# Weight bounds over partitions: a way through DRAM and VectorE in place of a GpSimd reduction

## The chip, the cores and the metric

One core of a Trainium2 chip runs the whole kernel. The metric is the device time of one execution in microseconds. The engines are named as in the profile: PE is TensorE's matmul, PEld its weight load, DVE is VectorE, ACT is ScalarE, POOL is GpSimd, SP is SyncE, which here only issues DMAs.

## The reference

A block of a streaming encoder on 2048 tokens of width 1024: a norm, one wide projection, stick-breaking attention and latent attention beside each other, gates, an output projection, and a last norm.

```python
h = rmsnorm(x, norm_in_g[l])
proj = jnp.einsum("bsd,de->bse", h, w_in[l])
(q_sb, k_sb, v_sb, gate_sb, c_q, c_kv, k_rope, gate_mla, gate_logits) = jnp.split(proj, offsets, axis=-1)
o_sb = stick_breaking_attention(q_sb, k_sb, v_sb)
y_sb = jnp.einsum("bsc,cd->bsd", o_sb * jax.nn.silu(gate_sb), w_o_sb[l])
q = jnp.einsum("bsr,re->bse", rmsnorm(c_q, q_norm_g[l]), w_q_up[l])
kv = jnp.einsum("bsr,re->bse", rmsnorm(c_kv, kv_norm_g[l]), w_kv_up[l])
o_mla = chunk_causal_softmax_attention(q_full, k_full, v_mla)
y_mla = jnp.einsum("bsc,cd->bsd", o_mla * jax.nn.silu(gate_mla), w_o_mla[l])
g = jax.nn.sigmoid(gate_logits + b_gate[l])
merged = g[:, :, 0, :] * y_sb + g[:, :, 1, :] * y_mla
x = x + jnp.einsum("bsd,de->bse", merged, w_out[l])
return rmsnorm(x, norm_f_g)
```

Each of the two attentions has 8 heads of width 64; the latent one adds 32 rotated columns to queries and keys.

## The kernel before

Every matrix product is made of three float16 products: each operand is split into a high part and a low part (`split`, L135: ScalarE casts the high part, VectorE takes the difference), and `gemm` (L139) adds high times high, high times low and low times high. Float16 has a narrow range, so each weight block is scaled first. The scale is a power -1/2 of a bound of the block, and the bound must be one number for all 128 partitions.

`prep_w` (L109) prepares one weight block: it loads it in two pieces (L118), ScalarE squares it and sums along the rows (L120), `bound_of` (L94) makes the bound, and then the block is cast into high and low parts with the factor `gs` (L126 to L131). `prep_up` (L391) does the same for the two up-projections of the latent attention, and `tail_scale` (L604) makes only the bound, for the output weights. There are 18 bounds: four of stick-breaking blocks, four of the latent attention (`cq`, `qu`, `ck`, `kvu`), eight of gate blocks, and two of output weights (`wo`, `wout`).

In `bound_of` VectorE sums the partition's squares (L97) and multiplies by the largest squared gain (L99), GpSimd takes the maximum over all partitions (L100), VectorE guards it against zero (L101), GpSimd takes the power -1/2 (L102), and VectorE multiplies the two to the square root (L103). The same power on GpSimd (L92) serves every norm, in `inv_rms`.

The work runs in two streams, which the program interleaves as it is written. `dense_stream` (L643) walks through the projections, block after block, 16 blocks of 128 rows in each; it prepares the next weight block all at once after the third row block (L649). The other stream is the attention: 8 stick-breaking heads (`sb_units`), then 8 latent heads (`mla_units`). `PLAN` says how many row blocks of the dense stream go beside each head: 17 in each of the first eight, 8 in the next seven, 4 in the last. The first 16 row blocks are beside the first norm of the input (`norm_x`). At the end come the gated output projections (L796 on).

A scheduler in the compiler puts the instructions of each engine into an order, by its own estimate of when each is ready; on the chip each engine then takes its queue in that order and waits where something is late. SP's queue holds the weight loads and also the transposes of the attention weights (L254, `hlT` from `hl`), each of which waits for VectorE's low part (L350) and is waited for by TensorE's product with the values (L263). On VectorE the stick-breaking heads bring a scan (L343), a product (L346) and a difference (L350) for each chunk; GpSimd brings the two triangular selects (L334, L336) and the power of the norms, and it issues DMAs.

`normed_ct` (L358) projects to the latent width, and its norm's factor `f` is taken on GpSimd (L92) and then multiplied by `m14`, a multiple of the bound, on VectorE (L366).

Of the kernel before, what the change touches and what calls it, by code (L numbers as in the profile page):

```python
# [9 lines left out]
F32 = mybir.dt.float32  # L10
# [20 lines left out]
SCALES = ("g", 5)  # L31
# [5 lines left out]
def block_kernel(tc, x, norm_in_g, w_in, w_ck, b_gate, q_norm_g, w_q_up, kv_norm_g, w_kv_up,  # L37
# [11 lines left out]
    with ExitStack() as ctx:  # L49
# [44 lines left out]
        def bound_of(ss, g2, m, rm):  # L94
# [14 lines left out]
        def prep_w(src, kk, n, g, g2, name):  # L109
# [15 lines left out]
            bound_of(am[:, 0:kk // 2], g2, m, rm)  # L125
# [22 lines left out]
        with ExitStack() as tctx:  # L148
# [57 lines left out]
            def sb_prep(hp):  # L206
                wh, wl, m = prep_w(w_in[hp], KD, WB, g_in, g2_in, f"sb{hp}")
# [150 lines left out]
            def normed_ct(i, wh, wl, n, nk, m24, m14, cdim):  # L358
# [6 lines left out]
                inv_rms(ssq, 1.0 / cdim, EPS, f)  # L365
                V.tensor_tensor(out=f, in0=f, in1=m14, op=ALU.mult)  # L366
# [24 lines left out]
            def prep_up(w, kk, n, g, g2, name):  # L391
# [15 lines left out]
                bound_of(am[:, 0:2 * kk], g2, m, rm)  # L407
# [14 lines left out]
            def mq_prep():  # L422
                wh, wl, mcq = prep_w(w_in[4], KD, 384, g_in, g2_in, "cq")
                uh, ul, mq = prep_up(w_q_up, 3, 768, g_q, g2_q, "qu")
                m24, m14 = scaled(mcq, 2.0 ** -24, "cq24"), scaled(mcq, 2.0 ** -14, "cq14")
                return wh, wl, uh, ul, mq, m24, m14

            def mq_project(pre):
                wh, wl, uh, ul, mq, m24, m14 = pre
                first = lambda i: normed_ct(i, wh, wl, 384, 3, m24, m14, 384)[1] if i < NB else None  # L430
# [22 lines left out]
            def mk_prep(mq):  # L453
                wh, wl, mck = prep_w(w_ck, KD, 288, g_in, g2_in, "ck")
                uh, ul, mkv = prep_up(w_kv_up, 2, 1024, g_kv, g2_kv, "kvu")
                m24, m14 = scaled(mck, 2.0 ** -24, "ck24"), scaled(mck, 2.0 ** -14, "ck14")
# [12 lines left out]
                return wh, wl, uh, ul, m24, m14, fkn, fkr, mzc, mof  # L469

            def mk_project(pre):
                wh, wl, uh, ul, m24, m14, fkn, fkr = pre[0:8]
                def first(i):
                    if i == NB:
                        return None
                    ps, ct = normed_ct(i, wh, wl, 288, 2, m24, m14, 256)
# [84 lines left out]
            def gate_prep(b):  # L561
                c0 = b * WB
                wh, wl, m = prep_w(w_in[5 + b], KD, WB, g_in, g2_in, f"gt{b}")
# [294 lines left out]
```

## Time and profile before

| | us |
|---|---|
| median of 3 runs (2335.77 to 2342.42) | 2337.99 |
| the profiled execution | 2340.05 |
| its span | 2338.2 |
| PE busy | 1903.0 (81%) |
| DVE busy | 1583.1 (68%) |
| ACT busy | 1241.5 (53%) |
| POOL busy | 483.7 (21%) |

The span is the profiled execution from its first instruction to its last; the time around it is 1.85 us. Busy is the time in which an engine has an instruction under way; waiting, branching and issuing DMAs don't count. In the rows, what stands behind an arrow in square brackets is what ended the idle time before an instruction; "issue" is time in which the engine waited for nothing that the profile shows. PEclk is the granted share of TensorE's full clock.

### The profile page before, as it was taken

To read this page: it belongs to the slowest core of one execution; us is meant where nothing else is said; L and a number is where in the kernel's file an instruction comes from. 1 tells how busy PE (TensorE), PEld (TensorE's weight loads), DVE (VectorE), ACT (ScalarE), POOL (GpSimd) and SP (SyncE) were. 2 spreads that over 40 slices of the span, in tenths; PEclk is the share of its full clock that TensorE was granted. 3 is DMA by queue.
4 is the path that set the end of the run, shared out by engine and by line. 5 is a ranking of instruction groups with operands and counts; after the bars stand their busy time and mean duration, and the time that the engine had idled before them with its cause. 6 is when DMAs were issued, how large, how long until landed. Compare 5 with 4: busy or idle time off the path is not lost.

```text
span 2338.2 us, 41738 instructions
## 1 busy us (share of the span) xinstructions
PE 1903.0 (81%) x15520; PEld 1102.1 (47%) x15520; DVE 1583.1 (68%) x3018; ACT 1241.5 (53%) x2180; POOL 483.7 (21%) x1128
## 2 busy tenths in 40 slices
PE   4677778778876887878887979988798895999997
PEld 2344444444444544545454545555455553444443
DVE  3356677766876866979786766766477667676674
ACT  4454656454565656767664655766456556332221
POOL 1212323322212213342322212211122110000000
PEclk9888989899997989999999989999899897999999
DMA  7976777686998868868676979999999988877752
GB/s 199 217 166 122 157 142 151 123 148 119 188 180 179 177 156 172 168 132 167 132 159 122 196 161 170 219 208 224 178 186 173 219 192 185 237 197 203 201 153 73
DMA packets 918253, 400.48 MB, mean 171 GB/s; under 512 B 857120, under 2 KB 875040, under 8 KB 916000
## 3 DMA queue, kind: packets, MB, share of 16 engines
q1 hardware_dynamic: 895456, 338.53, 71.6%
q0 software_dynamic: 20480, 58.74, 9.4%
q8 instruction: 122, 2.00, 0.4%
q10 hardware_dynamic: 2112, 0.52, 0.1%
q14 instruction: 83, 0.68, 0.1%
HBM read 131.34 MB, written 71.83 MB: 87 GB/s over the span
## 4 chain that ended last, share of the span: by engine, by line
PE 28%; DMA 24%; issue 19%; DVE 16%; ACT 7%; POOL 4%; SPq 2%; POOLq 0%; DVEq 0%; ACTq 0%
DMA hlT<-hl 13%; PE z L307 5%; DVE U L343 4%; DMA rt<-r 4%; PE mm L142 3%; PE mm L143 3%; PE mm L144 3%; DVE B L346 2%; DMA utb<-hlb 2%; DVE hl L350 2%; PE yo L142 2%; PE yo L144 2%; PE yo L143 2%; ACT U L331 1%; PE y L142 1%
## 5 line engine op out<-in xcount | busy, mean ns | idle before, releaser
L142 PE MATMUL mm<-w,hT 128*128 128x384 f16 (+1 forms) x1792 | 604.9, 338 | 118.0 <-DVE r L137 39.8
L143 PE MATMUL mm<-w,hT 128*128 128x384 f16 (+1 forms) x1792 | 605.2, 338 | 0.4 <-DVE w L131 0.4
L144 PE MATMUL mm<-w,hT 128*128 128x384 f16 (+1 forms) x1792 | 604.0, 337 | 0.0
L307 PE MATMUL z<-kt,qt 128*128 128x512 f16 (+3 forms) x1280 | 318.6, 364 | 89.7 <-ACT B L332 31.9
L263 PE MATMUL av<-vt,hlT 128*128 128x64 f16 x2176 | 238.7, 198 | 181.7 <-DMA hlT<-hl 178.7
L343 DVE TENSOR_TENSOR_SCAN U<-U 128x1024 f32<-128x1024 f32 (+3 forms) x192 | 332.1, 1732 | 45.1 <-POOL U L334 33.2
L263 PEld LDWEIGHTS <-hlT 128*128 128x128 f16 x2176 | 202.0, 101 | 237.3 <-DMA hlT<-hl 216.8
L349 ACT CAST hl<-B 128x1024 f16<-128x1024 f32 (+3 forms) x192 | 153.0, 798 | 269.9 <-DVE B L346 165.6
L143 PEld LDWEIGHTS <-hT 128*128 128x128 f16 x1792 | 182.2, 102 | 215.7 <-issue 115.7
L142 PEld LDWEIGHTS <-hT 128*128 128x128 f16 x1792 | 182.5, 102 | 150.6 <-issue 21.3
L307 PEld LDWEIGHTS <-qt 128*128 128x128 f16 x1600 | 147.2, 101 | 214.0 <-issue 85.3
L144 PEld LDWEIGHTS <-hT 128*128 128x128 f16 x1792 | 182.7, 102 | 124.9 <-issue 23.6
L266 PE MATMUL av<-vt,hlT 128*128 128x64 f16 x2176 | 238.2, 197 | 0.0
L265 PE MATMUL av<-vt,hlT 128*128 128x64 f16 x2176 | 238.0, 197 | 0.0
L350 DVE TENSOR_TENSOR hl<-B,hl 128x1024 f16<-128x1024 f32 (+3 forms) x192 | 174.3, 911 | 53.4 <-ACT hl L349 52.9
L265 PEld LDWEIGHTS <-hlT 128*128 128x128 f16 x2176 | 201.6, 101 | 17.4 <-issue 1.7
L266 PEld LDWEIGHTS <-hlT 128*128 128x128 f16 x2176 | 201.9, 101 | 0.0
L346 DVE TENSOR_TENSOR B<-B,U 128x1024 f32<-128x1024 f32 (+3 forms) x192 | 175.5, 916 | 12.9 <-POOL B L336 3.8
L332 ACT ACTIVATE B<-z,zc 128x1024 f32<-128x1024 f32 (+3 forms) x192 | 166.4, 866 | 31.2 <-DVE hl L350 30.8
L331 ACT ACTIVATE U<-z,nzc 128x1024 f32<-128x1024 f32 (+3 forms) x192 | 166.3, 866 | 13.8 <-PE z L307 13.5
L544 ACT ACTIVATE U<-U,nb 128x1024 f32<-128x1024 f32 (+7 forms) x128 | 98.5, 770 | 130.4 <-DVE nb L538 121.8
L92 POOL TENSOR_TENSOR f<-f,mhalf 128x1 f32<-128x1 f32 x64 | 41.6, 653 | 504.7 <-DVE f L91 497.5
(230 smaller groups left out, 3394.1 us busy)
## 6 DMA issues: line engine op xcount, KB each, us to landing
gd<-go POOLq DMA_DIRECT2D x128, 192.0 KB, 3.9
wf<-in_w_in_dram SPq DMA_DIRECT2D x26, 768.0 KB, 6.0
gt<-gd SPq DMA_DIRECT2D x10, 1024.0 KB, 6.2
qkd<-rt POOLq DMA_DIRECT2D x32, 256.0 KB, 3.8
mqd<-rt SPq DMA_DIRECT2D x32, 256.0 KB, 2.8
qt<-mqd POOLq DMA_DIRECT2D x32, 256.0 KB, 4.8
wf<-in_w_out_dram SPq DMA_DIRECT2D x16, 512.0 KB, 5.5
xt<-in_x_dram SPq DMA_DIRECT2D x16, 512.0 KB, 3.7
```

Of the source, the lines that this page charges most:

```text
L142: T.matmul(out=ps, lhsT=xh(k), rhs=wh(k), start=(k == 0), stop=False)
L143: T.matmul(out=ps, lhsT=xh(k), rhs=wl(k), start=False, stop=False)
L144: last_pe[0] = T.matmul(out=ps, lhsT=xl(k), rhs=wh(k), start=False, stop=(k == kk - 1))
L263: T.matmul(out=av[:, 0:64], lhsT=t[:, j, :], rhs=v[:, 0:64], start=(first and j == 0), stop=False)
L265: T.matmul(out=av[:, 0:64], lhsT=t[:, j, :], rhs=v[:, 64:128], start=False, stop=False)
L266: T.matmul(out=av[:, 0:64], lhsT=t[:, nb + j, :], rhs=v[:, 0:64], start=False, stop=(last and j == nb - 1))
L307: last_pe[0] = T.matmul(out=z[:, s:s + c], lhsT=st, rhs=half[:, o + s // P:o + (s + c) // P, :].rearrange("p a b -> p (a b)"), start=(a == ...
L331: A.activation(out=U[:, 1:n + 1], in_=z[:, 0:n], func=AF.Sigmoid, scale=nzc)
L332: A.activation(out=B[:, 0:n], in_=z[:, 0:n], func=AF.Sigmoid, scale=zc)
L343: V.tensor_tensor_scan(out=U[:, 1:n + 1], data0=U[:, 1:n + 1], data1=U[:, 1:n + 1], initial=U[:, 0:1], op0=ALU.mult, op1=ALU.bypass)
L346: V.tensor_tensor(out=B[:, 0:n], in0=B[:, 0:n], in1=U[:, 0:n], op=ALU.mult)
L350: V.tensor_tensor(out=lo, in0=B[:, 0:n], in1=hi, op=ALU.subtract)
```

## The change

The maximum over partitions no longer runs on GpSimd. VectorE's 128 partial values are stored as one row to DRAM, the row is loaded back to all partitions (512 bytes in each, into the tile `wjunk`, which also takes the unused squares), and VectorE takes the maximum along it. `bound_of` is now a generator with three yields, so that store, load, maximum and power, and the rest are traced one row block of the dense stream apart; `pin` puts an instruction behind what was traced before it on its engine. `prep` only puts the work into a queue, `behind`, and the dense stream takes one stage of it after each row block. The first weight block is prepared in one go (`all_behind`). The bounds of the output weights start after gate block 4 and not after gate block 5. The factor `m14` is folded into the two constants of the norm (`norm_scales`).

```diff
-SCALES = ("g", 5)
+SCALES = ("g", 4)
...
-        def bound_of(ss, g2, m, rm):
+        def pin(ins):
+
+            return tc.keep_in_program_order(ins)
+
+        def bound_of(ss, g2, m, rm, name):
...
             V.tensor_reduce(out=m, in_=ss, axis=AX.X, op=ALU.add)
             if g2 is not None:
                 V.tensor_tensor(out=m, in0=m, in1=g2, op=ALU.mult)
-            G.partition_all_reduce(m, m, P, bass.bass_isa.ReduceOp.max)
+            d = dram.tile([1, P], F32, name=f"bd_{name}")
+            SP.dma_start(out=d.rearrange("a p -> p a"), in_=m)
+            yield
+            row = wjunk[:, 0:2 * P].bitcast(F32)
+            pin(SP.dma_start(out=row, in_=d.broadcast_to([P, P])))
+            yield
+            pin(V.tensor_reduce(out=m, in_=row, axis=AX.X, op=ALU.max))
             V.tensor_scalar(out=m, in0=m, scalar1=TINY, scalar2=None, op0=ALU.max)
             G.tensor_tensor(out=rm, in0=m, in1=mhalf, op=ALU.pow)
-            V.tensor_tensor(out=m, in0=m, in1=rm, op=ALU.mult)
+            yield
+            pin(V.tensor_tensor(out=m, in0=m, in1=rm, op=ALU.mult))
...
-            bound_of(am[:, 0:kk // 2], g2, m, rm)
+            yield from bound_of(am[:, 0:kk // 2], g2, m, rm, name)
...
+            def norm_scales(m, cdim, name):
+
+
+                c1 = const.tile([P, 1], F32, name=f"{name}c1")
+                c0 = const.tile([P, 1], F32, name=f"{name}c0")
+                V.reciprocal(out=c0, in_=scaled(m, 2.0 ** -14, name + "14"))
+                V.tensor_tensor(out=c0, in0=c0, in1=c0, op=ALU.mult)
+                V.tensor_scalar(out=c1, in0=c0, scalar1=1.0 / cdim, scalar2=None, op0=ALU.mult)
+                V.tensor_scalar(out=c0, in0=c0, scalar1=EPS, scalar2=None, op0=ALU.mult)
+                return scaled(m, 2.0 ** -24, name + "24"), c1, c0
...
-                inv_rms(ssq, 1.0 / cdim, EPS, f)
-                V.tensor_tensor(out=f, in0=f, in1=m14, op=ALU.mult)
+                inv_rms(ssq, c1, c0, f)
...
+            behind = deque()
+
+            def work_behind():
+
+                if behind and next(behind[0], behind) is behind:
+                    behind.popleft()
+
+            def all_behind():
+                while behind:
+                    work_behind()
+
+            def store(key):
+                pre[key] = yield from prepare[key[0]](key[1])
...
-                        pre[kind, b] = prepare[kind](b)
+                        behind.append(store((kind, b)))
...
-                prep(0)
                 for j, (kind, b) in enumerate(steps):
+                    while (kind[0:1] if kind[0] == "g" else kind, b) not in pre:
+                        work_behind()
                     w = pre[kind[0:1] if kind[0] == "g" else kind, b]
                     for i, _ in enumerate(project[kind](b, w)):
                         if i == 2:
                             prep(j + 1)
+                        work_behind()
                         yield
...
                     if (kind, b) == SCALES:
-                        scales()
+                        behind.append(scales())
                     if (kind, b) == ("ga", 7):
+                        all_behind()
                         W["o"] = resident(0, [(w_o_sb, W["s"][0]), (w_o_mla, W["s"][0])])
...
                 if i == FIRST:
                     prep(0)
+                    all_behind()
```

The scheduler makes a new order of the whole program. Three places follow, as the built programs have them; the changed program's line numbers are its own (its scan is L355, product L358, difference L362, `gs` L138, low part of the weights L143).

GpSimd at the start of the program before. `f` is a norm's factor, `m_sb_156` the first weight block's bound, an ISA row without names loads code:

```order
L92 ISA
L92 TENSOR_TENSOR f<-f,mhalf 128x1
L522 MEMSET mx 128x4 x6
L100 ISA
L100 ISA m_sb_156<-m_sb_156 128x1
L102 ISA
L102 TENSOR_TENSOR rm<-m_sb_156,mhalf 128x1
L92 TENSOR_TENSOR f<-f,mhalf 128x1 x6
L230 DMA vd_76<-r 256x1x256
```

The same place in the changed program:

```order
L92 ISA
L92 TENSOR_TENSOR f<-f,mhalf 128x1
L543 MEMSET mx 128x4 x6
L92 TENSOR_TENSOR f<-f,mhalf 128x1 x5
L113 TENSOR_TENSOR rm<-m_sb_156,mhalf 128x1
L92 TENSOR_TENSOR f<-f,mhalf 128x1 x3
L242 DMA vd_76<-r 256x1x256
```

The reduction and the code rows on both sides of it are gone, here and at the other 17 bounds, and five powers of the input norm now stand ahead of the first bound's power.

VectorE at gate block 3 before, with heads of the stick-breaking attention beside it:

```order
L97 TENSOR_REDUCE m_gt_12198<-am 128x1
L99 TENSOR_TENSOR m_gt_12198<-m_gt_12198,g_in 128x1
L101 TENSOR_SCALAR m_gt_12198<-m_gt_12198 128x1
L343 SCALAR_TENSOR_TENSOR U<-U 128x1024
L103 TENSOR_TENSOR m_gt_12198<-m_gt_12198,rm 128x1
L126 TENSOR_SCALAR gs<-g_in,rm 128x8
L350 TENSOR_TENSOR hl<-B,hl 128x1024
L375 TENSOR_SCALAR gt_12234<-m_gt_12198 128x1
```

The same bound in the changed program, from the maximum along the row on; its partial value (L102, L104) stands 56 rows earlier:

```order
L602 SCALAR_TENSOR_TENSOR go<-mm,gt_11198,bt 128x128
L111 TENSOR_REDUCE m_gt_12211<-wjunk 128x1
L112 TENSOR_SCALAR m_gt_12211<-m_gt_12211 128x1
L355 SCALAR_TENSOR_TENSOR U<-U 128x640
L138 TENSOR_SCALAR gs<-g_in,rm 128x8
L358 TENSOR_TENSOR B<-B,U 128x640
L355 SCALAR_TENSOR_TENSOR U<-U 128x512
L143 SCALAR_TENSOR_TENSOR w<-wf,gs,w 128x384 x2
L358 TENSOR_TENSOR B<-B,U 128x512
L143 SCALAR_TENSOR_TENSOR w<-wf,gs,w 128x384 x6
L602 SCALAR_TENSOR_TENSOR go<-mm,gt_11198,bt 128x128
L115 TENSOR_TENSOR m_gt_12211<-m_gt_12211,rm 128x1
```

Before, the two lines that need GpSimd's results stand right behind the partial value, with one scan between them; now some fifty rows of other work lie between the partial value and the maximum, and one scan between the maximum's guard and the line that needs the power (L138).

SP in the changed program around the store and the load of the bound `kvu`, one of the six where they stand close; `hlT`, `ct` and `rt` are transposes that TensorE or stores wait for:

```order
L392 DMA_TRANSPOSE ct_7137<-c_7134 128x6x128
L470 DMA mqd1_81<-rt_6879 512x1x256
L266 DMA_TRANSPOSE hlT_7079<-hl_7076 128x16x128
L469 DMA_TRANSPOSE rt_7019<-r_7008 128x8x128
L106 DMA bd_kvu_5945<-m_kvu_5931 128x1
L266 DMA_TRANSPOSE hlT_7102<-hl_7099 128x2x128
L109 DMA wjunk_122<-bd_kvu_5945 128x128
L470 DMA mqd0_80<-rt_7019 512x1x256
```

Neither the store (L106) nor the load (L109) was in SP's queue before; here one transpose stands between them, and at twelve of the bounds 10 rows or more.

## Rows read from the trace of the kernel before

**Rows 1.** The page, part 1: engine, busy us, share, instructions.
```profile
PE 1903.0 (81%) x15520; PEld 1102.1 (47%) x15520; DVE 1583.1 (68%) x3018; ACT 1241.5 (53%) x2180; POOL 483.7 (21%) x1128
```

**Rows 2.** Line L100: durations (min/median/max ns), idle before, who waited.
```profile
L100 POOL PARTITION_ALL_REDUCE m_gt<-m_gt x8: 377/378/378, 726.9 to 1681.8; - x8
...
  issue: 111.4, 17
...
  DVE m_gt L101: 39.3, 8
```

**Rows 3.** Line L102, the power: idle before it, who waited for it.
```profile
  issue: 125.2, 17
...
  DVE m_gt L103: 48.0, 8
```

**Rows 4.** Timeline of GpSimd at the first gate block: start, us, instruction, idle.
```profile
726.90 0.38 POOL L100 PARTITION_ALL_REDUCE m_gt<-m_gt  x1 [6.00 <-issue]
...
734.79 0.59 POOL L102 TENSOR_TENSOR rm<-m_gt,mhalf 128x1 f32<-128x1 f32 x1 [7.26 <-issue]
```

**Rows 5.** Timeline of VectorE at the same bound.
```profile
720.36 0.15 DVE L99 TENSOR_TENSOR m_gt<-m_gt,g_in 128x1 f32<-128x1 f32 x1
...
727.31 0.15 DVE L101 TENSOR_SCALAR m_gt<-m_gt 128x1 f32<-128x1 f32 x1 [4.56 <-POOL m_gt L100]
...
735.41 0.16 DVE L103 TENSOR_TENSOR m_gt<-m_gt,rm 128x1 f32<-128x1 f32 x1 [6.19 <-POOL rm L102]
```

**Rows 6.** Windows around eleven bounds, 131 to 1148 us: length, busy us, PEclk.
```profile
720.50:750.60 30.10, 17.85 (x135) 11.53 (x135) 15.07 (x39) 12.59 (x30) 6.48 (x17) 0.77 0.73 152
...
sum 333.10, PE 214.17 PEld 121.13 DVE 183.58 ACT 146.67 POOL 79.46; mean PE 19.47 PEld 11.01 DVE 16.69 ACT 13.33 POOL 7.22
```

**Rows 7.** The nine stretches between them, 103 to 1119 us, in the same columns.
```profile
750.60:850.00 99.40, 86.67 (x714) 54.50 (x712) 80.91 (x171) 67.15 (x134) 26.04 (x45) 0.95 0.82 181
...
sum 691.60, PE 586.51 PEld 359.69 DVE 551.04 ACT 439.85 POOL 206.32; mean PE 65.17 PEld 39.97 DVE 61.23 ACT 48.87 POOL 22.92
```

**Rows 8.** Windows around five later bounds, 1229 to 1708 us: the sum.
```profile
sum 145.70, PE 105.38 PEld 61.89 DVE 79.11 ACT 67.13 POOL 31.78; mean PE 21.08 PEld 12.38 DVE 15.82 ACT 13.43 POOL 6.36
```

**Rows 9.** The four stretches between those, 1152 to 1649 us: the sum.
```profile
sum 409.20, PE 370.52 PEld 231.87 DVE 302.11 ACT 258.23 POOL 89.19; mean PE 92.63 PEld 57.97 DVE 75.53 ACT 64.56 POOL 22.30
```

**Rows 10.** Timeline of the first 40 us, all engines.
```profile
0.80 0.40 SPq L72 DMA_DIRECT2D g_in<-in_norm_in_g_dram  x1
...
11.52 7.26 SPq L199 DMA_TRANSPOSE hT<-hl  x1
...
13.11 0.16 DVE L99 TENSOR_TENSOR m_sb<-m_sb,g_in 128x1 f32<-128x1 f32 x1
...
27.09 0.59 POOL L102 TENSOR_TENSOR rm<-m_sb,mhalf 128x1 f32<-128x1 f32 x1 [8.45 <-issue]
...
28.72 0.48 PE L142 MATMUL mm<-w,hT 128*128 128x384 f16 x1 [28.72 <-ACT w L130]
...
39.08 0.10 PEld L142 LDWEIGHTS <-hT 128*128 128x128 f16 x1 [4.17 <-DMA hT<-hlT]
```

**Rows 11.** Line L366, the multiply by m14: idle before its 32 instructions.
```profile
  POOL f L92: 19.1, 12
```

**Rows 12.** DMA issues: name, engine, count, KB each, median us to landing.
```profile
mqd<-rt SPq DMA_DIRECT2D x32, 256.0 KB, 2.8
...
hlT<-hl SPq DMA_TRANSPOSE x384, 4.6
```

**Rows 13.** Line L81, a reduction along the row.
```profile
L81 DVE TENSOR_REDUCE g_in<-g_int x1: 163/163/163, 2.6 to 2.6; 128x1 f32<-128x8 f32 x1
```

**Rows 14.** Line L334, GpSimd's first select: idle before it, us and times.
```profile
  ACT U L331: 200.3, 61
```

**Rows 15.** SP's own waits: line, releaser, us in total, times, longest.
```profile
SPq L254 <- DVE hl L350: 238.7, 86, 16.0
```

More of the change, by code (lines that the diff above doesn't have):

```diff
@@ L206, in sb_prep @@
             def sb_prep(hp):
-                wh, wl, m = prep_w(w_in[hp], KD, WB, g_in, g2_in, f"sb{hp}")
+                wh, wl, m = yield from prep_w(w_in[hp], KD, WB, g_in, g2_in, f"sb{hp}")
                 zc = const.tile([P, 1], F32, name=f"zc{hp}")
@@ L422, in mq_prep @@
             def mq_prep():
[L423 to L426, printed above, removed]
+                wh, wl, mcq = yield from prep_w(w_in[4], KD, 384, g_in, g2_in, "cq")
+                uh, ul, mq = yield from prep_up(w_q_up, 3, 768, g_q, g2_q, "qu")
+                return wh, wl, uh, ul, mq, *norm_scales(mcq, 384, "cq")
             def mq_project(pre):
-                wh, wl, uh, ul, mq, m24, m14 = pre
-                first = lambda i: normed_ct(i, wh, wl, 384, 3, m24, m14, 384)[1] if i < NB else None
+                wh, wl, uh, ul, mq, m24, c1, c0 = pre
+                first = lambda i: normed_ct(i, wh, wl, 384, 3, m24, c1, c0, 384)[1] if i < NB else None
                 nxt = first(0)
@@ L453, in mk_prep @@
             def mk_prep(mq):
-                wh, wl, mck = prep_w(w_ck, KD, 288, g_in, g2_in, "ck")
-                uh, ul, mkv = prep_up(w_kv_up, 2, 1024, g_kv, g2_kv, "kvu")
-                m24, m14 = scaled(mck, 2.0 ** -24, "ck24"), scaled(mck, 2.0 ** -14, "ck14")
+                wh, wl, mck = yield from prep_w(w_ck, KD, 288, g_in, g2_in, "ck")
+                uh, ul, mkv = yield from prep_up(w_kv_up, 2, 1024, g_kv, g2_kv, "kvu")
+                m24, c1, c0 = norm_scales(mck, 256, "ck")
                 mk = const.tile([P, 1], F32, name="mk")
@@ L475, in first @@
                         return None
-                    ps, ct = normed_ct(i, wh, wl, 288, 2, m24, m14, 256)
+                    ps, ct = normed_ct(i, wh, wl, 288, 2, m24, c1, c0, 256)
                     r = rows.tile([P, 1536], F16, name="r", tag="r", bufs=3)
@@ L562, in gate_prep @@
                 c0 = b * WB
-                wh, wl, m = prep_w(w_in[5 + b], KD, WB, g_in, g2_in, f"gt{b}")
+                wh, wl, m = yield from prep_w(w_in[5 + b], KD, WB, g_in, g2_in, f"gt{b}")
                 mf = scaled(m, 2.0 ** -24, f"gt24{b}")
@@ L617, in tail_scale @@
                 r = const.tile([P, 1], F32, name=f"r_{name}")
-                bound_of(am, None, m, r)
+                yield from bound_of(am, None, m, r, name)
                 V.tensor_scalar(out=r, in0=r, scalar1=WS, scalar2=None, op0=ALU.mult)
@@ L637, in scales @@
                 mow = const.tile([P, 1], F32, name="mow")
-                m_o, r_o = tail_scale([w_o_sb, w_o_mla], "wo")
-                m_w, r_w = tail_scale([w_out], "wout")
+                m_o, r_o = yield from tail_scale([w_o_sb, w_o_mla], "wo")
+                m_w, r_w = yield from tail_scale([w_out], "wout")
                 V.tensor_scalar(out=mow, in0=m_o, scalar1=m_w, scalar2=2.0 ** -56, op0=ALU.mult, op1=ALU.mult)
```

8 lines of the change are left out of this document (4 added, 4 removed).

## The prediction

> **What bounds the kernel now.** I read the page first. VectorE is busy 68% of the span and TensorE 81% [rows 1], so neither is full, and the question is where they stand still. The waits of GpSimd answer it. The instruction that takes the largest value over the partitions lasts 0.38 us, but GpSimd sat idle 111.4 us before 17 of the 18 of them, with no releaser that the profile names ("issue"), and another 125.2 us before 17 of the powers that follow [rows 2, 3]. That is 6.6 and 7.4 us each time: GpSimd changes its code (the program has an ISA row ahead of each, shown with the change) to take the maximum, and changes back for the power.
>
> GpSimd's idle time alone would cost nothing. But VectorE takes its instructions in order, and the two small ones of the bound stand right behind each other with hardly any other work between. The timeline of one bound, the first gate block's, shows it: VectorE has the per-partition value at 720.5 us, GpSimd's maximum starts at 726.9 and the power at 734.8, and VectorE sits idle 4.56 us before L101 and 6.19 us before L103 [rows 4, 5]. Over the eight gate blocks it waits 39.3 us at L101 and 48.0 us at L103 [rows 2, 3], so 10.9 us a bound.
>
> Then I asked what such a stop costs, since engines may catch up. I laid one window around each of eleven bounds of the stretch with heads 0 to 7, from VectorE's value to 15 us after the power's result was used, so that catching up is inside, and compared with the stretches between. In the windows VectorE is busy 183.58 of 333.10 us, in between 551.04 of 691.60, which is 0.797 [rows 6, 7]. Its work in the windows would have taken 183.58 / 0.797 = 230.4 us between: 102.7 us are lost, 9.3 a bound. The same for five bounds of the later heads: 79.11 of 145.70 against 302.11 of 409.20, or 0.738; 38.5 us lost, 7.7 a bound [rows 8, 9]. ScalarE's busy times give 102.5 and 39.3 us from the same rows. TensorE's give less, 80.5 and 29.3, but part of its busy time there is matmuls at a lower granted clock (0.77 in one window, 0.95 in the stretch behind it, of the full 2.4 GHz) [rows 6, 7], so I take that as the lower bound.
>
> **The change part by part.**
>
> *The maximum leaves GpSimd.* All 36 changes of its code after the first go; the order of the program shows it. Sixteen bounds give back 102.7 + 38.5 = 141 us (lower bound 110, by TensorE). The second bound has no comparable stretch beside it, so it gets the mean of the sixteen, 8.8, as 9 us (lower 7). Upper bound for all 18: every microsecond of VectorE's wait returns, 18 x 10.9 = 196 us.
>
> Here a rule speaks against the change. The row says that the reduction itself is 0.38 us [rows 2] and that its surroundings are dear. The Trainium skill, GPSIMD Engine Reference, section 4.1 (Engine selection), sends a reduction over partitions to GpSimd and not to VectorE, and section 3.2 gives as the reason that it needs no way through HBM. By that rule the swap removes 18 x 0.38 = 7 us of GpSimd, buys 36 transfers with it, and is a loss. The rows say that the stops around it are worth 150 us (141 + 9); I go by the rows, and the rule's outcome is priced among the rivals.
>
> *The first bound* sets when TensorE starts, at 28.72 us [rows 10]. Now VectorE's value is there at 13.27 us (13.11 + 0.16), but SP is busy with the first transpose until 18.78 (11.52 + 7.26) [rows 10]; the store goes after it. A store by SP lands 2.8 us after its issue, a transpose 4.6 [rows 12]; I use the two as the bounds for the store and the load of a bound. Store down at 21.6, load down at 24.4 to 26.2, then the reduction and the maximum with TINY (0.3 and 0.16 us): the power at 24.9 to 26.7 instead of 27.09. TensorE follows 1.63 us later (28.72 - 27.09): 26.5 to 28.3, so 0.4 to 2.2 us earlier. Before, it then waits 4.17 us for the second row block, whose power stood behind the code changes [rows 10]; most of that goes. Together 5 us (bounds 0 to 8).
>
> *m14 folded into the norm's constants.* 32 multiplies of VectorE go (0.16 us each, 5 us), and VectorE no longer waits at L366 for GpSimd's power, 19.1 us [rows 11]. Scaled as the stops were (8.8 lost of 10.9 idle, 0.81), at most 20 us; ScalarE still waits for that power, so I take 10 (0 to 20). The new constants cost eight small instructions, 1 us.
>
> *Added on VectorE:* 18 reductions over 128 values. The nearest row, 8 values, takes 0.163 us [rows 13]; I estimate 0.3 us: 5.4 us, times 0.81, 4 us.
>
> *Added on SP:* 36 issues of 0.40 us [rows 10], 14 us, past which the transposes of the attention weights are moved. SP waits for VectorE most of the time (238.7 us in 86 waits for one line alone) [rows 15], so I take 5 (0 to 14).
>
> *New wait at the row's load and at L111.* The store waits for VectorE's value, and behind it on SP stand the transposes that TensorE's value products need; the load waits until the store has landed. At twelve bounds 10 to 44 SP rows lie between store and load, and some tens of VectorE's between value and L111: covered. At six (the first two, the two up-projections', gate block 6's and w_out's) there are one or two. There SP may stand for 2.8 us and VectorE for 4.6 [rows 12]: 6 x 7.4 x 0.81 = 36 us at most, 0 at least; one transpose covers part of it, and I take 8. If the cover were gone everywhere, that is the second rival.
>
> *New wait for the power.* Between the maximum with TINY and its user L138 VectorE has none to nine rows, mostly with a scan or a product. GpSimd's power stands in its own order, behind selects that wait 3.3 us on the mean for ScalarE (200.3 us over 61) [rows 14]. So 0 to 3.3 us a bound, 0 to 48 us; it is nearest to the low end, since a scan covers the power itself, and I take 1 us each: 18 x 0.81 = 15.
>
> *Moved:* squares, casts and weight loads keep their number. The bounds of the output weights come 16 steps earlier, the block weights two to eight steps later, still before the block that needs them; nothing.
>
> Sum: 141 + 9 + 5 + 10 = 165 back; 1 + 4 + 5 + 8 + 15 = 33 new; 132 us net. The profiled execution took 2340.05 us: 2208. The median of the runs, 2337.99, is 2 us lower, so the forecast is **2206 us**.
>
> **The rivals.**
>
> *All the idle time returns.* 196 us for the bounds in place of 150 (141 + 9), the rest as above: 2206 - 46 = 2160 us. For it: TensorE's clock falls in the windows, and would not. Against it: the windows show VectorE catching up. 10%.
>
> *The row comes late at every bound*, because SP runs behind the order that the scheduler planned; then VectorE stands at L111 for one landing, 18 x 4.6 x 0.81 = 67 us in place of 8: 2265 us. For it: SP's long waits [rows 15]. Against it: the many rows between store, load and L111. 15%. The Trainium skill, DMA: Bandwidth & Descriptors, "Anatomy of one DMA", puts some 2 us of fixed time on every transfer, most of it the target's receipt, heaviest in HBM; two of them exposed each time would be 58 us and nearly the same result. The 2.8 us row agrees in size; that it is exposed no row can show.
>
> *Slower: the way through DRAM costs VectorE more than the code changes did.* One mechanism: store, load and SP's own wait before each of them end in VectorE's wait at L111. It decides where that wait passes (165 - 25) / (18 x 0.81) = 9.6 us a bound, 25 us being the other new costs. With 2.8 + 4.6 us of landings and two waits of SP of 2.8 us each (238.7 / 86) [rows 12, 15] it is 13.0, 190 us in all: with those 25 us, 50 more than comes back: 2388. Against it: each stage begins a whole row block after the last one. 4%. This is how it would end by the engine rule of GPSIMD Engine Reference quoted above.
>
> *No change.* If VectorE's 68% meant slack, the stops would be made up later, beyond my 15 us, and the time stays 2338. Against it: VectorE runs at 0.80 between the windows, not at 1. 4%.
>
> **How the numbers follow.** The forecast has 67%, the others 10, 15, 4 and 4. I call 0.3% of the time, 7 us, about what a measurement can tell from no change. Faster: the first three cases, 0.92; same 0.04; slower 0.04. The forecast's own bounds at their corners (back 117 to 224, new 5 to 103 us) lie outside what is likely together. The range runs from just below the first rival, 2155, past the second to 2275: it leaves out the last two rivals and the forecast's far corners, under 2 in 10.
>
> **What would show it.** Right: no idle GpSimd of 6 us or more without a named releaser; VectorE's waits before the three lines that replace L101 to L103 under 3 us a bound; TensorE's first matmul near 27 us; VectorE busy about 1583 / 2206, 72%; no row of VectorE waiting for GpSimd at L366. Wrong: VectorE waiting for the row's load or for the power by more than 5 us a bound (second or third rival), SP's transposes held by a bound's store, or VectorE as idle as before in the stretches around the bounds with other releasers named.

## The result and the profile after

| | before | after |
|---|---|---|
| median of 4 runs | 2340.2 | 2277.53 (2274.37 to 2287.51) |
| ratio | | 0.9736 [0.9694, 0.9778] |
| the profiled execution, its span | 2340.05, 2338.2 | 2275.32, 2273.5 |
| TensorE's mean granted clock, of 2.4 GHz | 0.928 | 0.939 |

The forecast was 2206 us with a range of 2155 to 2275. The kernel became faster, as forecast, by 62 us in place of 132; the median lies just above the range. In what follows a ratio times 2338 gives microseconds, so that runs beside different medians of before can be compared.

The page of after, first its part 1, then the chain's lines and two groups of part 5:

```profile
PE 1890.2 (83%) x15520; PEld 1100.9 (48%) x15520; DVE 1588.3 (70%) x3012; ACT 1239.4 (55%) x2180; POOL 492.0 (22%) x1110
...
DMA hlT<-hl 19%; PE z L319 6%; PE mm L156 4%; PE mm L155 4%; PE mm L154 4%; DMA rt<-r 4%; DVE U L355 3%; PE yo L154 2%; DMA utb<-hlb 2%; PE yo L156 2%; PE yo L155 2%; PE av L275 2%; PE y L154 2%; PE y L155 1%; PE y L156 1%
...
L275 PE MATMUL av<-vt,hlT 128*128 128x64 f16 x2176 | 244.6, 200 | 230.3 <-DMA hlT<-hl 221.8
...
L275 PEld LDWEIGHTS <-hlT 128*128 128x128 f16 x2176 | 205.1, 102 | 288.4 <-DMA hlT<-hl 270.9
```

The same two groups in the page of before:

```profile
L263 PE MATMUL av<-vt,hlT 128*128 128x64 f16 x2176 | 238.7, 198 | 181.7 <-DMA hlT<-hl 178.7
...
L263 PEld LDWEIGHTS <-hlT 128*128 128x128 f16 x2176 | 202.0, 101 | 237.3 <-DMA hlT<-hl 216.8
```

GpSimd's idle time without a releaser before the maximum and the power [rows 2, 3] is gone. TensorE waits more elsewhere: its value products wait 221.8 us for a transpose of the attention weights, 43 us more than before, and the weight loads of the same products 54 us more. The prediction had named this as a sign of being wrong ("SP's transposes held by a bound's store").

VectorE's three possible waits: before L111 for the row, and, lines further down, before L138 and L115 for the power.

```profile
L111 DVE TENSOR_REDUCE m_gt<-wjunk x8: 274/286/288, 739.8 to 1681.3; 128x1 f32<-128x128 f32 x8
...
  DMA wjunk<-bd_sb: 14.9, 3
  DMA wjunk<-bd_kvu: 9.4, 1
  DMA wjunk<-bd_wout: 8.6, 1
  DMA wjunk<-bd_qu: 8.2, 1
  DMA wjunk<-bd_gt: 4.7, 4
  DMA wjunk<-bd_ck: 4.2, 1
  DMA wjunk<-bd_wo: 3.9, 1
```

```profile
  POOL rm L113: 3.0, 6
```

```profile
  POOL rm L113: 1.7, 2
  POOL r_wout L113: 0.6, 1
```

The reduction takes 0.286 us. The power costs VectorE 5.3 us in the whole program (3.0 + 1.7 + 0.6). The row costs it 53.9 us (the sum of the seven lines). By the timeline 42.7 us of it fall on the six bounds whose store and load stand close together (5.25 and 8.09 at the first two, 8.21 at `qu`, 9.44 at `kvu`, 8.58 at `wout`, 3.11 at gate block 6), 11.2 on the twelve others.

Why the row is late, the DMA issues of the two lines show: us from issue to landing (min/median/max), first the 18 stores of L106, then the 18 loads of L109.

```profile
DMA to landing us min/median/max: 8.4/9.9/13.2
```

```profile
DMA to landing us min/median/max: 3.8/4.2/5.2
```

The load is as quick as a transpose. The store of 512 bytes, 4 from each partition, takes more than three times what a 256 KB store took [rows 12]. The profile has the landing of 15 of the 18 stores and of 15 loads.

One such stop, at the bound `kvu`. First the DMA view of the window 653 to 668 us: the mean busy tenths of the 16 DMA engines and their GB/s in 40 slices of 0.375 us, then issues with the median us to landing. Then SP's and VectorE's timelines.

```profile
DMA  9999999600000500000000000000000000001258
GB/s 151 220 227 185 184 244 148 133 0 0 0 0 0 44 0 0 0 0 0 0 0 0 0 0 0 0 0 0 0 0 0 0 0 0 0 8 45 86 167 250
...
wjunk<-bd_kvu SPq DMA_DIRECT2D x1, 64.0 KB, 5.2
...
bd_kvu<-m_kvu SPq DMA_DIRECT2D x1, 0.5 KB, 9.4
hlT<-hl SPq DMA_TRANSPOSE x1, 8.9
```

```profile
653.64 0.53 SPq L106 DMA_DIRECT2D bd_kvu<-m_kvu  x1
654.28 1.18 SPq L266 DMA_TRANSPOSE hlT<-hl  x1
663.09 0.33 SPq L109 DMA_DIRECT2D wjunk<-bd_kvu  x1
```

```profile
656.54 2.35 DVE L355 TENSOR_TENSOR_SCAN U<-U 128x1024 f32<-128x1024 f32 x1 [0.69 <-POOL U L346]
668.33 0.29 DVE L111 TENSOR_REDUCE m_kvu<-wjunk 128x1 f32<-128x128 f32 x1 [9.44 <-DMA wjunk<-bd_kvu]
```

The store is issued at 653.64 and lands 9.4 us later, at 663.0. The transpose issued behind it lands at nearly the same moment, 8.9 us after its issue, where the median of before is 4.6 [rows 12]. From 656 on the DMA engines show next to no packets: the time is not spent on moving bytes. SP, pinned to its order, issues nothing until the store has landed, the load follows at 663.09, and VectorE stands for 9.44 us. So a store costs in three places: SP's queue, VectorE at L111, and whoever waits for a transfer that was issued beside it. Of the DMAs of after, the 38 issued between the issue and the landing of one of those 15 stores landed on the mean after 9.4 us, the others after 4.8 (worked out from each DMA's issue and landing). GpSimd's DMAs are among the 38.

The start, from the timeline of 8 to 45 us:

```profile
18.68 0.51 SPq L106 DMA_DIRECT2D bd_sb<-m_sb  x1
...
28.89 0.34 SPq L109 DMA_DIRECT2D wjunk<-bd_sb  x1
...
33.17 0.29 DVE L111 TENSOR_REDUCE m_sb<-wjunk 128x1 f32<-128x128 f32 x1 [5.25 <-DMA wjunk<-bd_sb]
...
34.11 0.55 POOL L113 TENSOR_TENSOR rm<-m_sb,mhalf 128x1 f32<-128x1 f32 x1
...
35.89 0.80 PE L154 MATMUL mm<-w,hT 128*128 128x384 f16 x2 [35.89 <-ACT w L142]
```

TensorE starts 7.2 us later than before [rows 10], and not 0.4 to 2.2 earlier. The store went out when I said (18.68; SP was free at 18.78 in before), but it took 10.2 us until the load could be issued.

### The profile page after: what moved, and what is told of

It reads as the page before. It is cut to its first block, busy times and chain, and to the rows that moved or that the text cites. A ratio compares the mean times of both kernels' runs of the same rounds, so it can differ in the third digit from the quotient of the medians.

```text
span 2273.5 us, 41721 instructions
## 1 busy us (share of the span) xinstructions
PE 1890.2 (83%) x15520; PEld 1100.9 (48%) x15520; DVE 1588.3 (70%) x3012; ACT 1239.4 (55%) x2180; POOL 492.0 (22%) x1110
## 3 DMA queue, kind: packets, MB, share of 16 engines
q0 software_dynamic: 20480, 58.74, 10.2%
## 4 chain that ended last, share of the span: by engine, by line
PE 35%; DMA 33%; issue 11%; DVE 11%; ACT 5%; POOL 3%; SPq 1%; POOLq 0%; DVEq 0%; ACTq 0%
DMA hlT<-hl 19%; PE z L319 6%; PE mm L156 4%; PE mm L155 4%; PE mm L154 4%; DMA rt<-r 4%; DVE U L355 3%; PE yo L154 2%; DMA utb<-hlb 2%; PE yo L156 2%; PE yo L155 2%; PE av L275 2%; PE y L154 2%; PE y L155 1%; PE y L156 1%
## 5 line engine op out<-in xcount | busy, mean ns | idle before, releaser
L154 PE MATMUL mm<-w,hT 128*128 128x384 f16 (+1 forms) x1792 | 596.4, 333 | 70.8 <-ACT w L142 39.8
L155 PE MATMUL mm<-w,hT 128*128 128x384 f16 (+1 forms) x1792 | 596.8, 333 | 0.7 <-DVE w L143 0.7
L156 PE MATMUL mm<-w,hT 128*128 128x384 f16 (+1 forms) x1792 | 596.0, 333 | 0.0
L275 PE MATMUL av<-vt,hlT 128*128 128x64 f16 x2176 | 244.6, 200 | 230.3 <-DMA hlT<-hl 221.8
L355 DVE TENSOR_TENSOR_SCAN U<-U 128x1024 f32<-128x1024 f32 (+3 forms) x192 | 332.1, 1732 | 62.7 <-POOL U L346 31.8
L275 PEld LDWEIGHTS <-hlT 128*128 128x128 f16 x2176 | 205.1, 102 | 288.4 <-DMA hlT<-hl 270.9
L154 PEld LDWEIGHTS <-hT 128*128 128x128 f16 x1792 | 180.3, 101 | 163.0 <-issue 28.1
L155 PEld LDWEIGHTS <-hT 128*128 128x128 f16 x1792 | 180.4, 101 | 143.5 <-issue 42.3
L278 PE MATMUL av<-vt,hlT 128*128 128x64 f16 x2176 | 244.4, 199 | 0.0
L277 PE MATMUL av<-vt,hlT 128*128 128x64 f16 x2176 | 244.1, 199 | 0.0
L156 PEld LDWEIGHTS <-hT 128*128 128x128 f16 x1792 | 180.3, 101 | 120.9 <-issue 17.2
L362 DVE TENSOR_TENSOR hl<-B,hl 128x1024 f16<-128x1024 f32 (+3 forms) x192 | 174.3, 911 | 67.0 <-ACT hl L361 66.7
L277 PEld LDWEIGHTS <-hlT 128*128 128x128 f16 x2176 | 205.1, 102 | 16.2 <-issue 1.7
L278 PEld LDWEIGHTS <-hlT 128*128 128x128 f16 x2176 | 205.7, 102 | 0.0
L358 DVE TENSOR_TENSOR B<-B,U 128x1024 f32<-128x1024 f32 (+3 forms) x192 | 175.1, 914 | 11.1 <-POOL B L348 2.6
```

The costliest lines, as they stand in the source:

```text
L154: T.matmul(out=ps, lhsT=xh(k), rhs=wh(k), start=(k == 0), stop=False)
L155: T.matmul(out=ps, lhsT=xh(k), rhs=wl(k), start=False, stop=False)
L156: last_pe[0] = T.matmul(out=ps, lhsT=xl(k), rhs=wh(k), start=False, stop=(k == kk - 1))
L275: T.matmul(out=av[:, 0:64], lhsT=t[:, j, :], rhs=v[:, 0:64], start=(first and j == 0), stop=False)
L277: T.matmul(out=av[:, 0:64], lhsT=t[:, j, :], rhs=v[:, 64:128], start=False, stop=False)
L278: T.matmul(out=av[:, 0:64], lhsT=t[:, nb + j, :], rhs=v[:, 0:64], start=False, stop=(last and j == nb - 1))
```

## The experiments

Theories: the **store** (its 4-byte pieces are slow and slow others), against the **stops** (the code changes of GpSimd cost less than I worked out), against the **stages** (work moved between row blocks costs or gains by itself). Edits are against the changed kernel where nothing else is said, and `...` marks lines left out of them. The range in brackets behind a ratio is its 95% interval.

**No way through DRAM.** The store, the load and the maximum along the row go; the two yields stay. Each partition then keeps its own value as its bound, so this is not a complete kernel; it only prices the transport.

```diff
-            d = dram.tile([1, P], F32, name=f"bd_{name}")
-            SP.dma_start(out=d.rearrange("a p -> p a"), in_=m)
             yield
-            row = wjunk[:, 0:2 * P].bitcast(F32)
-            pin(SP.dma_start(out=row, in_=d.broadcast_to([P, P])))
             yield
-            pin(V.tensor_reduce(out=m, in_=row, axis=AX.X, op=ALU.max))
```

> The changed kernel without the way through DRAM: store, load and the maximum along the row are left out, so each partition keeps its own value as its bound; the stages stay. Theory 1 (the store of 128 four-byte pieces lands only after some 10 us, holds the transposes queued behind it and makes VectorE wait for the row): with it gone the forecast comes true, 2190 to 2215 us, VectorE's wait at the maximum's line 0 and TensorE's waits for the transposes of the attention weights back from 222 to about 180 us. Theory 2 (any way through DRAM costs it, two landings and SP's waits): the same here. Theory 3 (the stops on GpSimd were worth only half of what the windows said, since something else bounds the stretch): 2255 to 2270 us, 10 to 20 us under the changed kernel.

Measured: 0.9476 [0.9415, 0.9536], 122 us under before. The transport costs 61 us (0.9736 - 0.9476; some 17 either way by the two intervals); I had put it at 17 (4 + 5 + 8).

**The store in four pieces of 128 bytes.** VectorE turns the column of partial values into rows first.

```diff
...
-            SP.dma_start(out=d.rearrange("a p -> p a"), in_=m)
+            V.tensor_copy(out=turn[:, 0:1], in_=m)
+            V.transpose(out=turned, in_=turn)
+            for q in range(4):
+                SP.dma_start(out=d[:, 32 * q:32 * q + 32], in_=turned[32 * q:32 * q + 1, :])
```

> The changed kernel with the store in four pieces of 128 bytes (VectorE turns its column of 128 values in blocks of 32 by 32, and four small stores follow) and nothing else changed. Theory 1: the stores land in 2.5 to 4.6 us, the transposes behind them in their usual 4.5, and the time is 2205 to 2235 us. Theory 2 (it is the receipt of a write to DRAM, whatever its pieces): the landing stays at 8 to 10 us and the time at 2270 to 2290. Theory 3: 2260 to 2275.

Measured: 0.9552 [0.9517, 0.9588]. Two more VectorE instructions and three more issues a bound, and still 43 us faster than the change as it was made. This trace has no landing of these stores, but SP's timeline bounds it: the load, which needs all four, goes out 1.9 us after the last of them at the first bound and 1.8 us at `kvu`; in after these were 10.2 and 9.45 us. TensorE's value products wait 196.4 us for the transposes, in place of 221.8.

**The store issued by ScalarE.** `A.dma_start` in place of `SP.dma_start` in L106.

> The changed kernel with the 18 stores issued by ScalarE, so on its own DMA queue; load and transposes stay with SP. Theory 1, if the transposes are held because they stand behind the store in one queue: they land in their usual 4.5 us again, TensorE's waits for them fall by some 40 us, VectorE's wait for the row stays near 50, and the time is 2235 to 2260 us. If the small pieces slow all of the DMA engines instead, the landings stay late and the time is 2270 to 2285. Theory 3: 2270 to 2280.

Measured: 0.9692 [0.9653, 0.9732]; its interval overlaps that of after. The landing of these stores, and the page's group of the value products:

```profile
DMA to landing us min/median/max: 7.3/8.7/14.4
```

```profile
L275 PE MATMUL av<-vt,hlT 128*128 128x64 f16 x2176 | 243.1, 199 | 236.4 <-DMA hlT<-hl 235.1
```

On another engine's queue the stores are as slow, and SP's transposes are waited for no less (235.1 us; 221.8 in after). The 46 DMAs that SP and GpSimd issued beside one of ScalarE's stores landed after 8.4 us on the mean, the others after 4.9. So it is not SP's queue alone that makes a transpose late beside a store.

**The kernel before with an unread store.** In the first form the store reads `m` itself:

```diff
             if g2 is not None:
                 V.tensor_tensor(out=m, in0=m, in1=g2, op=ALU.mult)
...
+            SP.dma_start(out=d.rearrange("a p -> p a"), in_=m)
             G.partition_all_reduce(m, m, P, bass.bass_isa.ReduceOp.max)
```

> The kernel before, with the same 18 stores added and nobody reading them; the maximum stays on GpSimd. Theory 1: the store alone holds the transposes behind it, 18 times 2 to 4 us of TensorE's waiting, 2365 to 2400 us. Theory 2 (only the waits for landings cost): 2338 to 2346, the 18 issues being all that is new. Theory 3: the same as theory 2.

Measured: 1.0302 [1.0261, 1.0343]. This mixes two things, since GpSimd's maximum overwrites `m` and so waits for the store (84.4 us at nine bounds). The second form stores a copy, `mc`, that nobody overwrites:

> The kernel before, with the 18 four-byte stores added, each from a copy of the value, so that nothing waits for a store: neither a reader nor a writer of the same tile. Theory 1 with the store slowing all transfers beside it: those issued while one is under way land in 9 us and not in 5, and the time is 15 to 50 us over the kernel before. Theory 1 with only the waits for the row and the tile: within 6 us of the kernel before.

Measured: 1.0247 [1.0209, 1.0285], 58 us slower, 3.2 a store, though nobody waits for one; I had put it at 15 to 50. The landing of the stores; the group of the value products; and GpSimd's idle time before the power of this kernel, then of before:

```profile
DMA to landing us min/median/max: 7.5/8.3/14.3
```

```profile
L270 PE MATMUL av<-vt,hlT 128*128 128x64 f16 x2176 | 242.0, 199 | 226.2 <-DMA hlT<-hl 225.2
```

```profile
POOL rm L109 <- issue: 133.5, 15, 12.9
```

```profile
POOL rm L102 <- issue: 110.9, 15, 8.4
```

Here the store's harm stands by itself: transposes are waited for 225.2 us in place of 178.7, and even GpSimd's return to the power's code takes 22.6 us longer. Both go with the store; by what way a store reaches GpSimd's return to the power, no run shows. As in after, the 44 DMAs issued beside a store landed after 9.0 us on the mean, the others after 4.7.

**The same with 128-byte pieces.** The kernel before with the copy, the transpose and the four stores of the second experiment, again read by nobody.

> The kernel before with 18 stores that nobody reads, now in four pieces of 128 bytes each; VectorE makes a copy and a turn for each. Against the same with pieces of four bytes, which was 59 us slower than the kernel before. Theory 1 (the pieces of four bytes are what slows the transfers): within 10 us of the kernel before. Rival (any small write to DRAM does): 30 us slower or more.

Measured: 0.9976 [0.9946, 1.0007]. The page's group of the value products:

```profile
L274 PE MATMUL av<-vt,hlT 128*128 128x64 f16 x2176 | 241.1, 199 | 193.2 <-DMA hlT<-hl 186.9
```

Four stores of 128 bytes, with what prepares them, cost nothing that can be measured; one store of 128 times 4 bytes costs 58 us over 18 bounds. The two waits go back with the time: 186.9 us for the transposes (178.7 in before, 225.2 with the 4-byte store), and 105.9 us of GpSimd's idle time before 15 powers (110.9 and 133.5). So the store's pieces make the harm, not a write to DRAM as such. What no run separates is their size from their number and place: all 128 lie side by side in 512 bytes.

**GpSimd's maximum, in stages.** The old reduction in the new stages:

```diff
-            d = dram.tile([1, P], F32, name=f"bd_{name}")
-            SP.dma_start(out=d.rearrange("a p -> p a"), in_=m)
             yield
-            row = wjunk[:, 0:2 * P].bitcast(F32)
-            pin(SP.dma_start(out=row, in_=d.broadcast_to([P, P])))
+            G.partition_all_reduce(m, m, P, bass.bass_isa.ReduceOp.max)
             yield
-            pin(V.tensor_reduce(out=m, in_=row, axis=AX.X, op=ALU.max))
```

> The changed kernel with the maximum back on GpSimd and the stages kept: no store, no load, but 36 changes of GpSimd's code. If what the stops cost was VectorE's own waiting, the stages alone give it back: 2205 to 2240 us. If GpSimd's standstill of some 14 us a bound costs by itself (selects, powers and loads of queries behind it in order), 2260 to 2320 us.

Measured: 1.0031 [1.0006, 1.0056], outside both expectations. VectorE's waits show that the run did not do what I meant: the guard (L108) still waited 78.4 us for the maximum, the square root (L111) 15.2 us for the power, and `gs` (L134) this much:

```profile
  POOL rm L109: 71.3, 11
```

The scheduler had moved the unpinned lines forward again. So I pinned the guard and `gs` as well and put one more yield ahead of the square root:

> The maximum on GpSimd in stages, and now VectorE's lines that need GpSimd's results (the maximum with TINY, the square root, the factor) are pinned one or two row blocks later, so that VectorE does not stand for them. If what the stops cost was VectorE's own waiting, it goes: 90 to 140 us under the kernel before. If it is GpSimd's standstill of 14 us a bound, through the selects, powers and query loads queued behind it, at most 40 us under the kernel before.

Measured: 0.9752 [0.9708, 0.9796], 58 us. VectorE's waits, before the guard (L108) and the square root (L112), and GpSimd's idle time before the maximum (L106) and the power (L109):

```profile
  POOL m_sb L106: 10.3, 2
  POOL m_qu L106: 6.1, 1
```

```profile
  POOL rm L109: 20.9, 3
```

```profile
  issue: 70.7, 11
```

```profile
  issue: 72.9, 10
```

VectorE waits 37.3 us for GpSimd here (164.9 in the run before it), and yet the kernel gains 58 us, between the two expectations, and not 122. GpSimd still stands 143.6 us without a releaser, and selects, powers of norms and loads of queries are queued behind these stops. By the factor 0.81 VectorE's 37.3 us are worth 30 of the 64 us by which this run lies behind the one without transport. The other 34 may be GpSimd's stops; but orders moved the time by as much elsewhere, so this run doesn't show it. It does show that pinning and stages alone, with the maximum left on GpSimd, come as far as the change itself did (0.9736).

**Without stages.** `all_behind()` right after each block is queued, so that a block is prepared at once, as before: the change itself, then without the transport, then with 128-byte pieces.

```diff
                         behind.append(store((kind, b)))
+                        all_behind()
...
                         behind.append(scales())
+                        all_behind()
```

> The changed kernel with every weight block prepared at once, as before, and the way through DRAM kept: VectorE then waits at the maximum's line for the store (10 us) and the load (4 us) of each bound with little beside it. By theory 1, 18 times 10 us or more: 2340 to 2420 us, slower than the kernel before. If the scheduler finds other work for VectorE meanwhile, 2275 to 2300.

Measured: 0.9867 [0.9838, 0.9896]. VectorE waits for the row at 17 of the 18 bounds, first lines of L111:

```profile
  DMA wjunk<-bd_gt: 38.9, 7
  DMA wjunk<-bd_sb: 35.8, 4
```

With all lines it is 130.2 us. With the slow store the stages are worth 31 us. The time lies between the two expectations.

> The kernel without store, load and row maximum (each partition keeps its own value), and every weight block prepared at once. It tells what the stages are worth when nothing has to be waited for: if they only hide the transfers, within 15 us of the same kernel in stages, which was 120 us under the kernel before; if they also smooth the casts, squares and loads of a block, 25 us or more slower than that.

Measured: 0.9349 [0.9313, 0.9385], 152 us under before, and 30 us under the same with stages, where I had expected it level or slower. This one is not a complete kernel either.

> The changed kernel with the store in four pieces of 128 bytes, and every weight block prepared at once. With the four-byte store, the stages were worth about 1.3% (0.9867 of the kernel before without them, 0.9736 with them); without any transfer they cost about 1.3%. If the stages only hide transfers: VectorE now waits some 7 us a bound for store and load, and the time is 0.965 to 0.985 of the kernel before (with stages it was 0.955). If the stages themselves cost as much as they hide: 0.945 to 0.960.

Measured: 0.9485 [0.9465, 0.9504]; with stages it was 0.9552. Where the transport is cheap or absent, these stages cost 16 to 30 us. Against the same without stages and with 4-byte pieces (0.9867) it is 89 us faster, the third pair that changes the pieces: 43 us in stages, 63 in the kernel before (1.0247 against 0.9976), 89 here. Each is more than the 38 us that stages and order moved the time by in any run. SP's timelines show why. At the bounds where the load stands right behind the last store, it goes out 1.2 to 2.8 us after that store with 128-byte pieces (five bounds) and 7.6 to 10.1 us with 4-byte pieces (five bounds).

**The factor alone.** `norm_scales` and its use in the kernel before, nothing else.

> The kernel before with m14 folded into the norm's constants and nothing else changed. The prediction's term: 10 us faster (0 to 20). Rival: ScalarE still waits for the power of GpSimd, and the multiply was beside it: within 3 us.

Measured: 1.0002 [0.9975, 1.0028]: nothing, where I had put 10 us back.

**A matmul in place of the way through DRAM.** VectorE spreads each partition's value along a row, TensorE multiplies by the identity, and every partition has all 128 values in PSUM. The store, the load and the old maximum go:

```diff
...
+            ps = ps_av()[:, 0:P]
+            wide = wjunk[:, 0:2 * P].bitcast(F32)
+            V.tensor_scalar(out=wide, in0=ident, scalar1=0.0, scalar2=m, op0=ALU.mult, op1=ALU.add)
+            pin(T.matmul(out=ps, lhsT=wide, rhs=ident, start=True, stop=True))
+            V.tensor_reduce(out=m, in_=ps, axis=AX.X, op=ALU.max)
```

It stands behind the last yield ahead of the maximum, with the stages kept.

> The changed kernel with no transfer for the bound: VectorE spreads its 128 values along 128 columns, one float32 matmul with an identity brings them as a row to all partitions, and VectorE takes the maximum from PSUM; the stages stay. Theory 1 (the four-byte store is what the change gave back, by its landing of 10 us and by slowing every transfer beside it): within 15 us of the kernel without transport, 2205 to 2230, transfers landing as in the kernel before. Theory 2 (any way for the values to cross the partitions costs in-order waits): TensorE now waits for VectorE at 18 places, 2240 to 2265.

Measured: 0.9405 [0.938, 0.943], 139 us under before and faster than expected: the best complete version, ahead of both kernels, and between the two runs that have no transport at all (0.9476 and 0.9349). So these runs can't tell the matmul's price from nothing. The first bound in its timeline:

```profile
13.17 0.29 DVE L112 TENSOR_SCALAR wjunk<-ident,m_sb 128x128 f32<-128x128 f32 x1
...
13.60 0.77 PE L113 MATMUL av<-ident,wjunk 128*128 128x128 f32 x2 [13.60 <-DVE wjunk L112]
...
14.40 0.29 DVE L114 TENSOR_REDUCE m_sb<-av 128x1 f32<-128x128 f32 x1 [0.43 <-PE av L113]
...
14.96 0.55 POOL L116 TENSOR_TENSOR rm<-m_sb,mhalf 128x1 f32<-128x1 f32 x1 [0.35 <-DVE m_sb L115]
...
20.35 0.50 PE L157 MATMUL mm<-w,hT 128*128 128x384 f16 x1 [5.98 <-DMA hT<-hl]
```

From the partial value to the maximum in every partition it takes 1.52 us (13.17 to 14.69), where store and load take 14.8 (18.68 to 33.46). TensorE's first projection starts at 20.35 us, and what it waited for last is a transpose of the input, no longer the weights.

The same with `all_behind()` for all blocks but the latent ones:

> The bound over the partitions by one matmul, as before, but the weight blocks of the stick-breaking attention, the gates and the output weights' bounds prepared at once; only the latent attention's blocks stay in stages. In stages it was 0.9405 of the kernel before. If the stages cost by themselves what they cost the kernel without transport: 0.925 to 0.936, the fastest of all. If that difference was only the luck of one order: 0.936 to 0.950.

Measured: 0.9566 [0.954, 0.9592], outside both expectations. Here taking the stages away costs 38 us, the opposite of the two cases before. Each of these edits also makes the scheduler order the whole program anew. What a stage is worth by itself, apart from the order that came with it, stays open.

## Why the prediction was off, point by point

The direction and the larger term were right. The step that failed is the price of the row's way through DRAM: 17 us in the sum (4 + 5 + 8), 61 in the runs. Under it lies the reading "A store by SP lands 2.8 us after its issue, a transpose 4.6 [rows 12]; I use the two as the bounds for the store and the load of a bound", and a term that the sum does not have: what a store does to the transfers beside it.

- **What the stops give back.** Without the transport the forecast has 149 us left of its sum (165 back, 1 and 15 new). The two runs without it gave 122 (109 to 137 by the interval) with stages and 152 (144 to 161) without them. So the windows around the bounds, busy time against the rate in between [rows 6 to 9], priced the stops about right; the two orders of the program lie too far apart to say it more closely. The upper bound of 196 us took the gate blocks' 10.9 us for all 18 bounds; VectorE's waits at L101 and L103 add up to 187.5. Whether a stop also costs by what is queued behind GpSimd, which the prediction left out, the pinned run leaves open.
- **The store's landing.** Forecast 2.8 to 4.6 us, measured 8.4 to 13.2. No row of before shows a DMA with pieces of 4 bytes, and the two rows that I took as bounds are of a store with large pieces and of a transpose. The first has 512 times the bytes, which I let pass for a bound from above. The trace of before does have loads in small pieces, 8 to 32 bytes for each partition (L72 to L74), and they landed after 1.6 to 1.8 us: they go the other way, from DRAM, and would have misled as well. The Trainium skill, DMA: Bandwidth & Descriptors, "Anatomy of one DMA", gives for a DMA issued by GpSimd some 2 us of fixed time and then bytes over bandwidth; the prediction carried that over to SP's. The load of the row, 4.2 us, took about twice that, the store four to over six times. The measurements decide.
- **What else waits.** I looked for the cost at SP and at L111 alone. A store delays the transfers issued beside it, 9.4 us against 4.8, whatever queue issued it. Of the 70 us by which the forecast missed, 43 are the pieces of the store (0.9736 against 0.9552). The other 18 us of the transport are near the 17 that I had worked out for all of it. The remaining 27 are the first point's 149 against 122 in the staged order, 10 of them m14's. The intervals leave 13 to 17 us either way on each part; what makes the 17 us beside m14 stays open.
- **The cover of the row.** I took the wait to be covered at twelve bounds and worth 8 us at the six close ones, 36 at most. VectorE waited 42.7 us at the six, which is 35 by the factor 0.81 that I used there, and 11.2 us at the twelve. The place was right; in the range that I had given, the upper end was the one to take.
- **The first bound.** TensorE 7.2 us later and not up to 2.2 earlier, by the same store. The working was also short of its own bounds: it took 2.8 us for the store at both ends. With 4.6 for store and load TensorE starts at 30.1 us, 1.4 later than before.
- **m14.** 10 us forecast, 0 measured (7 us either way at most). The idle time before L366 [rows 11] did not set the end; scaling it as the stops were scaled had no row behind it.
- **The reduction and the power.** The reduction was put at 0.3 us and took 0.286. VectorE's wait for the power was put at 18 us (15 in the sum) and was 5.3, inside its bounds and near their low end.
- **Stages costing nothing.** Not so: between 38 us won and 30 lost, together with the order that came with them.

Of the rivals, the row that comes late, 2265 us, came nearest in time. Its reason was another: not SP running behind its order, but a store that lands late. The slower rival needed 9.6 us a bound at L111; it was 3.0 (53.9 / 18). By the Trainium skill's GPSIMD Engine Reference, section 4.1, GpSimd is the engine for a reduction over partitions. The runs decide against it here: every complete version that left GpSimd for it was faster than before, from 0.9867 to 0.9405. But the version that keeps GpSimd and pins the users of its results later (0.9752) is level with the change as it was made (0.9736).

## What to carry to other kernels

Price a transfer by a row with the same size of piece and the same direction, not by one with more bytes; where the trace has none, leave the upper end open or give the step a run of its own. For 128 values that every partition needs, one matmul with the identity was the shortest of the ways tried here (1.52 us, no DMA); in the kernel's time the order decided as much, for it gave 0.9405 in stages and 0.9566 mostly without, where the 128-byte pieces gave 0.9552 and 0.9485. A stop's cost is better read by comparing busy rates around it with those between (150 us for all the stops, where the runs without transport gave back 122 and 152) than from one engine's waits (187.5 us at two lines). Before moving work off an engine, try what pinning the lines that wait for it gives.

## What the runs showed that I had not expected

- A DMA of 128 pieces of 4 bytes from SBUF to DRAM lands after 6.7 to 14.4 us, on SP's queue or on ScalarE's. In the window shown the DMA engines' records have next to no packets for most of that time. Other DMAs issued meanwhile land in about twice their usual time. Four DMAs of 128 bytes cost nothing that could be measured. What inside the chip holds them was not settled.
- An unread store that nobody waits for slowed the kernel before by 58 us [49, 67] over 18 bounds.
- Taking the stages away cost up to 38 us in one version and gave back 30 in another, what the edit does and the order that the scheduler then made taken together. So a run that edits a few lines tests the new order as well.
